# Two products a weight block for the queries, the memory keys and the convolution input, with a PSUM bank for each half

## The chip, the core and the metric

The kernel runs on one core of one Trainium2 chip. The core has a matrix engine (TensorE, PE in the profile), a vector engine (VectorE, DVE), a scalar engine (ScalarE, ACT), a general engine (GpSimd, POOL) and DMA queues, most of them issued by SyncE (SP). Each engine works through its own queue in order, and semaphores tie the queues together. Matrix products land in PSUM, eight banks of 512 fp32 columns a partition; everything else lives in SBUF. The metric is the time of one execution on the device, in microseconds (us), smaller being better.

## The reference: a trunk of two layers

A sequence of 256 tokens of width 1024 goes through two layers. Each layer has four steps, each followed by a layer norm of the sum with the residual:

```
x <- LN(alpha*x + 0.5*SwiGLU_1(x))
x <- LN(alpha*x + W_o( sum_b sigmoid(G_b x) * (y_b W_b) ))     b in {retention, DSA, NSA, SSD}
x <- LN(alpha*x + CrossAttn(x, mem))                           4 heads, 256 memory tokens
x <- LN(alpha*x + 0.5*SwiGLU_2(x))
```

Three places matter here. The cross attention projects queries from `x` and keys from `mem`, both 1024 wide. The SSD mixer takes 768 of its input columns through a causal convolution of four taps and a SiLU:

```
q = (x @ wq).reshape(B, S, X_HEADS, X_DH)
kv = (mem @ wkv).reshape(B, M, 2, X_HEADS, X_DH)
xbc = silu(conv(xbc, conv_w) + conv_b)
```

The NSA mixer compresses its keys into 15 blocks and scores every query of four heads against them:

```
p_cmp = masked_softmax(jnp.einsum('bshd,bcd->bhsc', q, k_cmp) * scale, cmp_visible[None, None])
```

Everything is fp32, and the kernel has to keep close to fp32 precision.

## The kernel before

**Precision by halves.** TensorE multiplies numbers of a reduced type (`F32R`) in one pass. The kernel therefore writes every operand as a high part and a low part: ScalarE copies the number into the reduced type (`wH`, line 177; line 207 for activations), VectorE subtracts that from the original (`wL`, line 178; line 208). A product is the sum of high by high, high by low and low by high. The helper `mm3` (lines 188 to 193) issues these as three matmuls into one PSUM region.

**Weights.** All weights stream once from HBM, most of the 267 MB read, in chunks of 1 MB. `chunk_hl` issues the load into one of three `raw` buffers, and splits it in two halves of 128 x 1024, each into a `wH` and a `wL` from a pool that holds four such pairs, that is, two chunks. So a later chunk's split has to wait until TensorE has used up a half two chunks earlier, and its load until a `raw` buffer is free.

**Units.** The work of TensorE is cut into generators, "units", each of which uses one weight chunk. The next unit's chunk is loaded and split while the current one multiplies. Between units' pieces, the small steps of the token mixers, of the attention heads and of the layer norms are woven in. A scheduler at build time then sets the order of instructions in each engine's queue; it is fixed when the kernel runs.

**Features by tokens.** `feat2` (line 417) computes 256 output features for 256 tokens, as two feature tiles `ft` of 128 rows. Both go into one PSUM bank of the pair called `mm`: columns 0 to 255 for the first, 256 to 511 for the second. For each tile there are eight weight blocks of 128 x 128, and for each block three matmuls of 256 columns: `wH` by `xH` (line 191), `wH` by `xL` (192), `wL` by `xH` (193). When both tiles are done, the bank is read once. Four kinds of unit use it. In a layer there are

- four memory-key units (`kv_unit`, line 440, for i < 4), whose bank ScalarE copies into `kT` (line 200);
- four `query` units (line 537), whose bank ScalarE scales into `qH` (line 544) and VectorE reads again for `qL` (line 545);
- three `conv` units (line 1023), whose bank ScalarE copies into `xp` (line 200); VectorE then computes the taps into `cu` (lines 1036 and 1038), ScalarE a tanh (`cth`, 1040), VectorE the result `xc` (1042);
- sixteen gate units, which the change doesn't touch.

The memory-key units fill TensorE while a layer norm runs on VectorE: four in the first norm of layer 0, and for layer 1 two each in the third and fourth norms of layer 0. In the cross attention each query unit is followed by a head's steps, woven into the next query's: scores into a bank of the pair `tp` (`tp<-xkH,qH` and its like), softmax, transposes and values.

The feed-forward units have another form (lines 369 and 370): `xH` and `xL` lie beside each other in the tile `xP`, so `wH` is multiplied with both in one matmul of 512 columns, and `wL` by `xH` is added to the first 256. The bank then holds two halves, which ScalarE copies (374) and VectorE adds (375).

**Scores on compressed keys.** In `nsa` the compressed keys `kcT` are one fp32 tile of 128 x 16, and each of eight matmuls (two token tiles, four heads; line 979) is a full fp32 product, whose result VectorE adds to a mask (line 985).

**Around the convolution.** The SSD mixer's scan is woven into the convolution units. There TensorE multiplies a table `sA` with ones (line 1095), VectorE turns a column of that into `ncs` (1088, 1105), and TensorE adds a mask to the same bank (1109), for which it waits for `ncs`.

Of the kernel before, what the change touches and what calls it, by code (L numbers as in the profile page):

```python
# [9 lines left out]
F32 = mybir.dt.float32  # L10
F32R = mybir.dt.float32r
BF16 = mybir.dt.bfloat16
AF = mybir.ActivationFunctionType
# [3 lines left out]
S = 256  # L17
# [121 lines left out]
class Trunk:  # L139
# [277 lines left out]
    def feat2(self, sp, x, first=None):  # L417
# [8 lines left out]
                    yield  # L426
        return b


    def load_mem(self, pool, tag="mem"):  # L430
        both = pool.tile([128, 2, 8, S], F32R, name="mem", tag=tag, bufs=1)
        self.memH, self.memL = both[:, 0], both[:, 1]
        r = self.rawp.tile([128, 2048], F32, name="raw")
        self.nc.sync.dma_start(r, self.a["memT"])
        for i in range(2):
            sl = slice(4 * i, 4 * i + 4)
            self.hl_from(self.memH[:, sl].rearrange("p a b -> p (a b)"),
                         self.memL[:, sl].rearrange("p a b -> p (a b)"), r[:, i * 1024:(i + 1) * 1024])

    def kv_unit(self, l, i):  # L440

        if i == 0:
            self.kT = self.big.tile([128, 8, S], F32, name="kT")
            self.vM = self.big.tile([128, 2, D], F32, name="vM")
        mem = lambda k, sl=slice(0, S): (self.memH[:, k, sl], self.memL[:, k, sl])
        sp = self.chunk_hl(l, "kv"[i // 4], i % 4)
        yield
        if i < 4:
            b = yield from self.feat2(sp, mem)
            self.evac(self.kT[:, 2 * i:2 * i + 2, :].rearrange("p a b -> p (a b)"), b, eng="act")  # L450
            return
        hf, part = divmod(i - 4, 2)
        if part == 0:
            self.vacc = [self.mmb() for _ in range(2)]
        for kk in range(4):
            k = part * 4 + kk
            w = tuple(p[:, (kk % 2) * 512:(kk % 2) * 512 + 512] for p in sp[kk // 2])
            for t in range(2):
                self.mm3(self.vacc[t], mem(k, slice(t * 128, t * 128 + 128)), w, k == 0, k == 7)
            yield  # L460
        if part == 1:
            for t in range(2):
                self.evac(self.vM[:, t, hf * 512:hf * 512 + 512], self.vacc[t], eng="act")
# [73 lines left out]
    def query(self, l, h, wk):  # L537
        nc = self.nc
        sp = self.chunk_hl(l, "q", h)
        yield  # L540
        b = yield from self.feat2(sp, self.x_hl)
        self.q[h] = [wk[0].tile([128, 2, S], F32R, name="q" + n) for n in "HL"]
        qH, qL = (w.rearrange("p a b -> p (a b)") for w in self.q[h])
        nc.scalar.activation(qH, b, AF.Copy, scale=1.0 / 16.0)
        nc.vector.scalar_tensor_tensor(qL, b, 1.0 / 16.0, qH.bitcast(F32), op0=OP.mult, op1=OP.subtract)

    def token_acc(self, acc, blocks, first, last):

# [368 lines left out]
    def nsa(self, mp):  # L917
# [46 lines left out]
        nc.tensor.matmul(cp[0][:, :16], w2r.rearrange("p a b -> p (a b)"), x[:, 0, :], start=True, stop=True)  # L964
        nc.tensor.matmul(cp[1][:64, :64], rep.rearrange("p a b -> p (a b)"), w2, start=True, stop=True)

        kcT = self.sm.tile([128, 16], F32, name="kcT", bufs=1)
        nc.scalar.activation(kcT, cp[0][:, :16], AF.Copy)
        vb = mp.tile([128, 4, 64], F32, name="vblk", bufs=1)
        nc.gpsimd.memset(vb[64:], 0.0)  # L970
        bm = self.c("blkm", 64)
# [3 lines left out]
        sc = self.acc()  # L975
        for t in range(2):
            for h in range(4):
                c = (t * 4 + h) * 16
                nc.tensor.matmul(sc[:, c:c + 16], nqT[t][:, h].bitcast(F32), kcT, start=True, stop=True)
        pc = self.sm.tile([128, 2, 4, 16], F32, name="pc", bufs=1)  # L980
        mx = self.sm.tile([128, 8], F32, name="pcm", bufs=1)
        sm = self.sm.tile([128, 8], F32, name="pcs", bufs=1)
        cm = self.c("cmpm").rearrange("p (t o c) -> p t o c", t=2, o=1)
        pc3 = pc.rearrange("p t h c -> p (t h) c")
        nc.vector.tensor_tensor(pc, sc[:, :128].rearrange("p (t h c) -> p t h c", t=2, h=4), cm.to_broadcast([128, 2, 4, 16]), OP.add)
        nc.vector.tensor_reduce(mx, pc3, axis=AX, op=OP.max)
        nc.vector.tensor_scalar(mx, mx, -0.1 * BIG, None, op0=OP.max)
        nc.vector.tensor_tensor(pc3, pc3, mx[:, :, None].to_broadcast([128, 8, 16]), OP.subtract)
# [34 lines left out]
    def conv(self, l, i, mp):  # L1023

        nc = self.nc
        sp = self.chunk_hl(l, "xbc", i)
        yield
        b = yield from self.feat2(sp, self.x_hl)
        xp = mp.tile([128, 2, S + 3], F32, name="xp", tag="t2")
        nc.gpsimd.memset(xp[:, :, :3], 0.0)  # L1030
        self.evac(xp[:, :, 3:], b.rearrange("p (a n) -> p a n", a=2), eng="act")
        u = mp.tile([128, 2, S], F32, name="cu", tag="t2")
        cw = self.cwh[:, :24].rearrange("p (f j) -> p f j", f=6)
        for a in range(2):
            f = 2 * i + a
            nc.vector.tensor_scalar(u[:, a], xp[:, a, 3:], cw[:, f, 3:4], self.cwh[:, 24 + f:25 + f], op0=OP.mult, op1=OP.add)
            for j in range(3):
                nc.vector.scalar_tensor_tensor(u[:, a], xp[:, a, j:j + S], cw[:, f, j:j + 1], u[:, a], op0=OP.mult, op1=OP.add)
        th = mp.tile([128, 2, S], F32, name="cth", tag="t2")
        nc.scalar.activation(th, u, AF.Tanh)  # L1040
        xc = mp.tile([128, 2, S], F32, name=f"xc{i}", bufs=1)
        nc.vector.scalar_tensor_tensor(xc, th, 1.0, u, op0=OP.add, op1=OP.mult)
        self.xc[i] = xc
        if i == 2:
            self.done.add("xbc")
# [383 lines left out]
```

## Time and profile before

| | us |
|---|---|
| median of three runs | 1471.2 |
| lowest and highest run | 1469.06, 1472.23 |
| profiled execution | 1470.16 |
| its span, first to last instruction | 1468.4 |
| TensorE busy | 1451.9 (99%) |
| VectorE busy | 1059.1 (72%) |
| ScalarE busy | 800.4 (55%) |
| GpSimd busy | 126.1 (9%) |

The granted TensorE clock was 0.998 of full speed over the span. The busy time of a matmul in the profile includes its way through a pipeline, so matmuls overlap: 128 x 256 products are listed with some 0.28 us and start 0.12 us apart. What a stream of them costs is read from start to start. An idle time in brackets is that of the engine before the instruction, with what ended it.

### The profile page before, as it was taken

The page shows a single profiled execution, that of the slowest core. Times are in us where ns is not written, and L with a number is a line of the kernel's source. Part 1 is how long each engine was busy: PE and PEld are TensorE (multiplying, and loading weights), DVE is VectorE, ACT ScalarE, POOL GpSimd, SP SyncE. Part 2 cuts the span into 40 slices and gives each one's busy share as a digit, 9 for nine tenths or more (in the row PEclk, how much of TensorE's full clock was granted, in tenths as well). Part 3 has the DMA queues.
Part 4 walks back from the last instruction along what each step waited for, and adds up shares of the span by engine and source line. Part 5 has one row for each costly group of instructions (what it writes and reads, how often), then busy time and mean ns, then how long its engine had stood idle before and what let it go on. Part 6 is the DMA issues. An engine that isn't in the chain of part 4 may idle for free.

```text
span 1468.4 us, 22627 instructions
## 1 busy us (share of the span) xinstructions
PE 1451.9 (99%) x8949; PEld 1292.0 (88%) x8949; DVE 1059.1 (72%) x1671; ACT 800.4 (55%) x1302; POOL 126.1 (9%) x130
## 2 busy tenths in 40 slices
PE   8999999999999999999999999999999999999997
PEld 6888899899997988888898888898999979888886
DVE  7666668887768777666676566789877788676665
ACT  6555546645654546555546565466556546365552
POOL 0000002301421000000000000023014210000000
PEclk9999999999999999999999999999999999999999
DMA  8576555543454636555556555454333555365550
GB/s 311 190 275 237 189 165 188 172 132 128 144 187 183 234 144 227 186 210 191 190 176 224 191 209 179 179 200 172 121 139 144 192 180 203 115 230 182 208 184 29
DMA packets 40857, 269.38 MB, mean 183 GB/s; under 512 B 4528, under 2 KB 4784, under 8 KB 10288
## 3 DMA queue, kind: packets, MB, share of 16 engines
q1 hardware_dynamic: 40176, 266.89, 51.4%
q8 instruction: 70, 1.15, 0.3%
q10 hardware_dynamic: 576, 1.05, 0.2%
q14 instruction: 35, 0.29, 0.1%
HBM read 266.88 MB, written 1.05 MB: 182 GB/s over the span
## 4 chain that ended last, share of the span: by engine, by line
PE 96%; DVE 1%; DMA 1%; ACT 1%; POOL 0%; issue 0%; DVEq 0%; ACTq 0%
PE tp L369 11%; PE mm L369 11%; PE acc L193 10%; PE acc L191 10%; PE acc L192 10%; PE mm L191 8%; PE mm L192 8%; PE mm L193 8%; PE mm L370 5%; PE tp L370 5%; PE tp L327 1%; PE tp L192 1%; PE tp L681 1%; PE tp L193 1%; PE tp L191 1%; PE tp L603 1%
## 5 line engine op out<-in xcount | busy, mean ns | idle before, releaser
L178 DVE TENSOR_TENSOR wL<-raw,wH 128x1024 fp32r<-128x1024 f32 (+2 forms) x478 | 585.3, 1233 | 235.4 <-ACT wH L177 231.6
L177 ACT ACTIVATE wH<-raw 128x1024 fp32r<-128x1024 f32 (+2 forms) x478 | 496.1, 1048 | 300.4 <-PE mm L192 127.3
L369 PE MATMUL mm<-xP,wH 128*128 128x512 f32 x704 | 249.4, 394 | 1.8 <-DVE xP L208 1.8
L369 PE MATMUL tp<-xP,wH 128*128 128x512 f32 x704 | 249.1, 394 | 0.0
L191 PE MATMUL mm<-xP,wH 128*128 128x256 f32 x736 | 213.9, 291 | 0.3 <-ACT vM L200 0.3
L192 PE MATMUL mm<-xP,wH 128*128 128x256 f32 x736 | 208.5, 283 | 0.0
L193 PE MATMUL mm<-xP,wL 128*128 128x256 f32 x736 | 208.0, 283 | 0.0
L370 PE MATMUL mm<-xP,wL 128*128 128x256 f32 x704 | 195.7, 278 | 0.5 <-DVE wL L178 0.5
L370 PE MATMUL tp<-xP,wL 128*128 128x256 f32 x704 | 195.4, 278 | 0.0
L369 PEld LDWEIGHTS mm<-xP,wH 128*128 128x128 f32 x704 | 132.0, 187 | 33.6 <-ACT wH L177 2.5
L369 PEld LDWEIGHTS tp<-xP,wH 128*128 128x128 f32 x704 | 132.0, 188 | 30.7
L191 PEld LDWEIGHTS mm<-xP,wH 128*128 128x128 f32 x736 | 140.6, 191 | 2.3 <-ACT vM L200 1.4
L192 PEld LDWEIGHTS mm<-xP,wH 128*128 128x128 f32 x736 | 140.6, 191 | 1.4 <-issue 0.6
L193 PEld LDWEIGHTS mm<-xP,wL 128*128 128x128 f32 x736 | 140.6, 191 | 0.1
L192 PE MATMUL acc<-wL,hH 128*128 128x512 f32 x352 | 137.8, 392 | 0.0
L191 PE MATMUL acc<-wH,hH 128*128 128x512 f32 x352 | 137.7, 391 | 0.0
L193 PE MATMUL acc<-wH,hL 128*128 128x512 f32 x352 | 137.5, 391 | 0.0
L370 PEld LDWEIGHTS mm<-xP,wL 128*128 128x128 f32 x704 | 132.3, 188 | 5.0 <-DVE wL L178 1.6
L370 PEld LDWEIGHTS tp<-xP,wL 128*128 128x128 f32 x704 | 132.3, 188 | 0.0
L374 ACT ACTIVATE g<-mm 128x256 f32<-128x256 f32 x88 | 33.7, 383 | 111.4 <-PE mm L370 111.3
L375 DVE TENSOR_TENSOR g<-mm,g 128x256 f32<-128x256 f32 x88 | 37.2, 423 | 75.2 <-ACT g L374 75.2
L193 PE MATMUL acc<-wH,xP 128*128 128x512 f32 (+1 forms) x224 | 85.0, 379 | 1.9 <-POOL xP L1198 1.9
(332 smaller groups left out, 2385.8 us busy)
## 6 DMA issues: line engine op xcount, KB each, us to landing
raw<-in_w_dram SPq DMA_DIRECT2D x232, 1024.0 KB, 4.9
raw<-in_memT_dram SPq DMA_DIRECT2D x5, 1024.0 KB, 4.8
lnG<-in_ln_g_dram SPq DMA_DIRECT2D x8, 512.0 KB, 3.8
lnB<-in_ln_b_dram SPq DMA_DIRECT2D x8, 512.0 KB, 5.1
raw<-in_w_dram SPq DMA_DIRECT2D x4, 624.0 KB, 3.9
w<-in_w_dram SPq DMA_DIRECT2D x8, 256.0 KB, 4.8
raw<-in_w_dram SPq DMA_DIRECT2D x4, 256.0 KB, 6.2
raw<-in_xT_dram ACTq DMA_DIRECT2D x4, 256.0 KB, 6.6
```

The lines of the kernel that those rows point to most:

```text
L177: self.nc.scalar.activation(h, src, AF.Copy)
L178: self.nc.vector.tensor_tensor(lo, src, h.bitcast(F32), OP.subtract)
L191: mm(out, a[0], b[0], start=start, stop=False, **kw)
L192: mm(out, a[0], b[1], start=False, stop=False, **kw)
L193: mm(out, a[1], b[0], start=False, stop=stop, **kw)
L327: nc.tensor.transpose(p[:, k * 128:k * 128 + 128], X[:, t, (h * 4 + k) * 128:(h * 4 + k + 1) * 128], self.ident)
L369: nc.tensor.matmul(b[s], w[0][:, off:off + 128], self.xP[:, :, k], start=k == 0, stop=False, skip_group_check=True)
L370: nc.tensor.matmul(b[s][:, :256], w[1][:, off:off + 128], self.xH[:, k], start=False, stop=k == 7, skip_group_check=True)
L374: nc.scalar.activation(g[:, s], b[s][:, 256:], AF.Copy)
L375: nc.vector.tensor_tensor(g[:, s], b[s][:, :256], g[:, s], OP.add)
L603: self.nc.tensor.transpose(p[:parts, i * 128:i * 128 + 128].bitcast(F32R), v, self.identr)
L681: nc.tensor.transpose(b[:, h * 128:h * 128 + 128], ps[h // hb][:, h % hb, j * 128:j * 128 + 128], self.ident)
```

## The change

A new generator `feat_apart` takes the place of `feat2` for memory keys, queries and convolution inputs. It gives each of the two feature tiles a whole `mm` bank, and uses two matmuls a weight block, in the form of the feed-forward units: 512 columns of `[xH | xL]` with `wH`, and 256 columns of `xH` with `wL`. After each feature tile the bank's two halves are put together by `both`: ScalarE copies the one, VectorE adds the other. For queries this goes into one small fp32 buffer `half`, which is then split into `qH` and `qL` as any other activation. The compressed keys are split as well: the scores have `F32R` operands and 32 columns (16 high, 16 low), and a second VectorE operation adds the two.

```diff
+    def feat_apart(self, sp, xP, evac):
+        nc = self.nc
+        for ft in range(2):
+            b = self.mmb()
+            for k in range(8):
+                h, lo = (p[:, k * 128:k * 128 + 128] for p in sp[ft])
+                nc.tensor.matmul(b, h, xP[:, :, k], start=k == 0, stop=False, skip_group_check=True)
+                nc.tensor.matmul(b[:, :256], lo, xP[:, 0, k], start=False, stop=k == 7, skip_group_check=True)
+                if k == 7:
+                    evac(ft, b[:, :256], b[:, 256:])
+                if k % 4 == 3:
+                    yield
+
+    def both(self, out, high, low, scale=1.0):
+        self.nc.scalar.activation(out, low, AF.Copy, scale=scale)
+        self.nc.vector.scalar_tensor_tensor(out, high, scale, out, op0=OP.mult, op1=OP.add)
...
         if i < 4:
-            b = yield from self.feat2(sp, mem)
-            self.evac(self.kT[:, 2 * i:2 * i + 2, :].rearrange("p a b -> p (a b)"), b, eng="act")
+            kT = self.kT[:, 2 * i:2 * i + 2]
+            yield from self.feat_apart(sp, self.memP, lambda ft, b, lo: self.both(kT[:, ft], b, lo))
             return
...
         sp = self.chunk_hl(l, "q", h)
         yield
-        b = yield from self.feat2(sp, self.x_hl)
-        self.q[h] = [wk[0].tile([128, 2, S], F32R, name="q" + n) for n in "HL"]
-        qH, qL = (w.rearrange("p a b -> p (a b)") for w in self.q[h])
-        nc.scalar.activation(qH, b, AF.Copy, scale=1.0 / 16.0)
-        nc.vector.scalar_tensor_tensor(qL, b, 1.0 / 16.0, qH.bitcast(F32), op0=OP.mult, op1=OP.subtract)
+        def evac(ft, b, lo):
+            if ft == 0:
+                self.q[h] = [wk[0].tile([128, 2, S], F32R, name="q" + n) for n in "HL"]
+            t = self.sm.tile([128, S], F32, name="half", bufs=1)
+            self.both(t, b, lo, 1.0 / 16.0)
+            self.hl_from(*(w[:, ft] for w in self.q[h]), t)
+
+        yield from self.feat_apart(sp, self.xP, evac)
...
-        kcT = self.sm.tile([128, 16], F32, name="kcT", bufs=1)
-        nc.scalar.activation(kcT, cp[0][:, :16], AF.Copy)
+        kcT = self.sm.tile([128, 2, 16], F32R, name="kcT", bufs=1)
+        self.hl_from(kcT[:, 0], kcT[:, 1], cp[0][:, :16])
...
-                c = (t * 4 + h) * 16
-                nc.tensor.matmul(sc[:, c:c + 16], nqT[t][:, h].bitcast(F32), kcT, start=True, stop=True)
+                c = (t * 4 + h) * 32
+                nc.tensor.matmul(sc[:, c:c + 32], nqT[t][:, h], kcT.rearrange("p a c -> p (a c)"), start=True, stop=True)
...
-        nc.vector.tensor_tensor(pc, sc[:, :128].rearrange("p (t h c) -> p t h c", t=2, h=4), cm.to_broadcast([128, 2, 4, 16]), OP.add)
+        scv = sc[:, :256].rearrange("p (t h a c) -> p t h a c", t=2, h=4, a=2)
+        nc.vector.tensor_tensor(pc, scv[:, :, :, 0], cm.to_broadcast([128, 2, 4, 16]), OP.add)
+        nc.vector.tensor_tensor(pc, scv[:, :, :, 1], pc, OP.add)
...
-        b = yield from self.feat2(sp, self.x_hl)
         xp = mp.tile([128, 2, S + 3], F32, name="xp", tag="t2")
         nc.gpsimd.memset(xp[:, :, :3], 0.0)
-        self.evac(xp[:, :, 3:], b.rearrange("p (a n) -> p a n", a=2), eng="act")
+        yield from self.feat_apart(sp, self.xP, lambda ft, b, lo: self.both(xp[:, ft, 3:], b, lo))
```

In the changed file the two matmuls are lines 437 and 438 and the two operations of `both` lines 445 and 446; later lines move by 22 to 24, so that what was line 1038 is 1062, and 1105 is 1129.

Since the scheduler sets the order again, rows move beside each other. The first place is VectorE's queue at the first two queries of layer 0. Before, from the split of the first head's keys and values on:

```order
L208 TENSOR_TENSOR xvL<-vM,xvH 128x512
L178 TENSOR_TENSOR wL<-raw,wH 128x1024 x2
L545 SCALAR_TENSOR_TENSOR qL<-mm,qH 128x512
L178 TENSOR_TENSOR wL<-raw,wH 128x1024 x2
L488 TENSOR_REDUCE xnm<-tp 128x2
```

After, from the same row on:

```order
L208 TENSOR_TENSOR xvL<-vM,xvH 128x512
L178 TENSOR_TENSOR wL<-raw,wH 128x1024
L446 SCALAR_TENSOR_TENSOR half<-mm,half 128x256
L178 TENSOR_TENSOR wL<-raw,wH 128x1024
L208 TENSOR_TENSOR qL<-half,qH 128x256
L178 TENSOR_TENSOR wL<-raw,wH 128x1024
L446 SCALAR_TENSOR_TENSOR half<-mm,half 128x256
L178 TENSOR_TENSOR wL<-raw,wH 128x1024
L208 TENSOR_TENSOR qL<-half,qH 128x256
```

One operation of a query has become four, with splits of weights between them. ScalarE's queue at the same place, before:

```order
L207 ACTIVATE xkH<-kT 128x512
L207 ACTIVATE xvH<-vM 128x512
L177 ACTIVATE wH<-raw 128x1024 x2
L544 ACTIVATE qH<-mm 128x512
L177 ACTIVATE wH<-raw 128x1024 x3
```

And after:

```order
L207 ACTIVATE xkH<-kT 128x512
L207 ACTIVATE xvH<-vM 128x512
L177 ACTIVATE wH<-raw 128x1024
L445 ACTIVATE half<-mm 128x256
L177 ACTIVATE wH<-raw 128x1024
L207 ACTIVATE qH<-half 128x256
L177 ACTIVATE wH<-raw 128x1024
L445 ACTIVATE half<-mm 128x256
L177 ACTIVATE wH<-raw 128x1024 x2
```

The second copy out of a bank now comes after the third of these splits, where the one copy of before came after the second. The last place is VectorE's queue at the first convolution unit of layer 0, before:

```order
L202 CAST iqT<-tp 128x512
L178 TENSOR_TENSOR wL<-raw,wH 128x1024
L1088 TENSOR_SCALAR ncs<-acc 128x8
L1105 TENSOR_TENSOR ncs<-acc,ncs 128x4
L1036 TENSOR_SCALAR cu<-xp,cwh 128x256 x2
L1038 SCALAR_TENSOR_TENSOR cu<-xp,cwh,cu 128x256 x6
```

And after:

```order
L202 CAST iqT<-tp 128x512
L178 TENSOR_TENSOR wL<-raw,wH 128x1024
L446 SCALAR_TENSOR_TENSOR xp<-mm,xp 128x256
L1112 TENSOR_SCALAR ncs<-acc 128x8
L1129 TENSOR_TENSOR ncs<-acc,ncs 128x4
L1060 TENSOR_SCALAR cu<-xp,cwh 128x256
L1062 SCALAR_TENSOR_TENSOR cu<-xp,cwh,cu 128x256 x2
L446 SCALAR_TENSOR_TENSOR xp<-mm,xp 128x256
L1062 SCALAR_TENSOR_TENSOR cu<-xp,cwh,cu 128x256
L1060 TENSOR_SCALAR cu<-xp,cwh 128x256
L178 TENSOR_TENSOR wL<-raw,wH 128x1024
```

The add of the first feature tile stands ahead of `ncs`, and the taps of that tile no longer wait for the second one.

## Rows read from the trace of the kernel before

**Rows 1.** Page: busy time of each engine, and the chain by engine.

```profile
PE 1451.9 (99%) x8949; PEld 1292.0 (88%) x8949; DVE 1059.1 (72%) x1671; ACT 800.4 (55%) x1302; POOL 126.1 (9%) x130
...
PE 96%; DVE 1%; DMA 1%; ACT 1%; POOL 0%; issue 0%; DVEq 0%; ACTq 0%
```

**Rows 2.** By stretch: length; PE, PEld, DVE, ACT, POOL busy; clock; DMA share, GB/s.

```profile
546.00:559.00 13.00, 13.00 (x111) 12.91 (x111) 12.63 (x21) 5.72 (x8) 1.85 (x2) 1.00 0.30 89
...
226.00:262.00 36.00, 35.74 (x242) 32.86 (x241) 31.78 (x69) 22.39 (x41) 9.65 (x10) 1.00 0.46 150
...
487.00:520.00 33.00, 33.00 (x269) 32.26 (x268) 25.55 (x38) 23.15 (x40) 0.00 (x0) 1.00 0.51 182
1208.00:1241.00 33.00, 32.70 (x266) 31.73 (x265) 28.53 (x40) 22.77 (x40) 0.00 (x0) 1.00 0.65 228
```

**Rows 3.** Timeline of PE (start, duration, operation): old triples, query and memory.

```profile
488.21 0.28 PE L191 MATMUL mm<-xP,wH 128*128 128x256 f32 x1
...
493.60 0.28 PE L191 MATMUL mm<-xP,wH 128*128 128x256 f32 x1
...
204.06 0.28 PE L191 MATMUL mm<-mem,wH 128*128 128x256 f32 x1
...
215.06 0.28 PE L191 MATMUL mm<-mem,wH 128*128 128x256 f32 x1
```

**Rows 4.** Timeline of PE: pairs of two feed-forward units.

```profile
64.17 0.39 PE L369 MATMUL tp<-xP,wH 128*128 128x512 f32 x1
...
66.59 0.40 PE L369 MATMUL tp<-xP,wH 128*128 128x512 f32 x1
...
755.31 0.39 PE L369 MATMUL mm<-xP,wH 128*128 128x512 f32 x1
...
758.14 0.40 PE L369 MATMUL tp<-xP,wH 128*128 128x512 f32 x1
```

**Rows 5.** Timeline of PE: compressed scores, and neighbours of 256 columns.

```profile
346.03 0.28 PE L649 MATMUL acc<-keyH,qT 128*128 128x256 f32 x1
346.15 0.28 PE L650 MATMUL acc<-keyL,qT 128*128 128x256 f32 x1
...
346.74 1.85 PE L979 MATMUL acc<-kcT,qT 128*128 128x16 f32 x16
348.44 0.36 PE L191 MATMUL mm<-xP,wH 128*128 128x256 f32 x1
```

**Rows 6.** Page, costliest groups: busy us, mean ns of one, idle before.

```profile
L178 DVE TENSOR_TENSOR wL<-raw,wH 128x1024 fp32r<-128x1024 f32 (+2 forms) x478 | 585.3, 1233 | 235.4 <-ACT wH L177 231.6
L177 ACT ACTIVATE wH<-raw 128x1024 fp32r<-128x1024 f32 (+2 forms) x478 | 496.1, 1048 | 300.4 <-PE mm L192 127.3
...
L374 ACT ACTIVATE g<-mm 128x256 f32<-128x256 f32 x88 | 33.7, 383 | 111.4 <-PE mm L370 111.3
L375 DVE TENSOR_TENSOR g<-mm,g 128x256 f32<-128x256 f32 x88 | 37.2, 423 | 75.2 <-ACT g L374 75.2
```

**Rows 7.** Timeline of ACT at the first two queries of either layer.

```profile
493.68 1.06 ACT L177 ACTIVATE wH<-raw 128x1024 fp32r<-128x1024 f32 x1 [1.82 <-PE mm L192]
...
495.46 3.11 ACT L177 ACTIVATE wH<-raw 128x1024 fp32r<-128x1024 f32 x3 [0.23 <-DMA raw<-in_w_dram]
...
1216.88 1.06 ACT L177 ACTIVATE wH<-raw 128x1024 fp32r<-128x1024 f32 x1 [1.77 <-PE mm L192]
...
1218.77 2.96 ACT L177 ACTIVATE wH<-raw 128x1024 fp32r<-128x1024 f32 x3 [0.35 <-DMA raw<-in_w_dram]
```

**Rows 8.** Timeline of PE and DVE at the first convolution unit, layer 0.

```profile
240.56 0.38 PE L1109 MATMUL acc<-lowb,nident 128*128 128x512 bf16 x1 [0.26 <-DVE ncs L1105]
...
242.64 0.74 DVE L1036 TENSOR_SCALAR cu<-xp,cwh 128x256 f32<-128x256 f32 x2 [2.13 <-ACT xp L200]
```

**Rows 9.** Timeline of DVE at the norm's end; PE's waits, sum, times, longest.

```profile
558.38 1.29 DVE L208 TENSOR_TENSOR xP<-tp,xP 128x512 fp32r<-128x512 f32 x2 [0.29 <-ACT xP L207]
...
PE mm L369 <- DVE xP L208: 1.8, 3, 0.8
```

More of the change, by code (lines that the diff above doesn't have):

```diff
@@ L427, in feat2 @@
         return b
+    def feat_apart(self, sp, xP, evac):
[13 more added lines that the diff above has]
+        self.nc.vector.scalar_tensor_tensor(out, high, scale, out, op0=OP.mult, op1=OP.add)
     def load_mem(self, pool, tag="mem"):
         both = pool.tile([128, 2, 8, S], F32R, name="mem", tag=tag, bufs=1)
-        self.memH, self.memL = both[:, 0], both[:, 1]
+        self.memP, self.memH, self.memL = both, both[:, 0], both[:, 1]
         r = self.rawp.tile([128, 2048], F32, name="raw")
```

## The prediction

> **What bounds the kernel now.** I read the page's totals first, then the chain of work that ended last, then the stages in which the changed units run. TensorE is busy 99% of the span and makes up 96% of the chain [rows 1]: it is the bound, and it runs its queue in a fixed order. So only two things move the time: how long the matmul queue is, and where its head has to wait. VectorE, at 72%, has room on average; but the change puts work on it in four kinds of stage, and there the room differs [rows 2]: 28.5 of 33 us in the queries of layer 1, 25.6 of 33 in those of layer 0, 31.8 of 36 in the convolution, 12.6 of 13 in the norm beside which two memory-key units run. Those stages decide.
>
> **What it takes from TensorE.** Busy times of matmuls overlap, so I cost a block by its start-to-start distance. The old three products of 256 columns over xP: 15 blocks lie between the query's first complete block at 488.21 and the next query's first at 493.60, 5.39/15 = 359 ns [rows 3]. The same over the memory: 31 blocks from 204.06 to 215.06, 11.00/31 = 355 ns [rows 3]. The new form, one product of 512 columns and one of 256, is what the feed-forward units already do: 7 blocks from 64.17 to 66.59 give 346 ns, 8 from 755.31 to 758.14 give 354 [rows 4]. The form is the same, the place differs, so I take the middle, 350. Fourteen units over xP (8 queries, 6 convolution inputs) of 16 blocks save 224 x 9 ns = 2.0 us (1.1 at 354, 2.9 at 346); eight memory-key units save 128 x 5 ns = 0.6 us (0.1 to 1.2).
>
> The scores on compressed keys: 16 records start between 346.74 and 348.44, 1.70 us a layer, two records for each of the 8 fp32 matmuls [rows 5]. With split keys 8 single products are left. At the same 106 ns apiece they cost 0.85, and their neighbours with 256 columns, 120 ns apart [rows 5], bound them by 0.96: 0.85 less a layer, 1.7 in all (1.5 to 1.9). The split of the keys (one more small VectorE operation) and the second add hang on a woven chain with two yields before its matmuls; I cost them at nothing, and if that cover is gone, at two small operations of some 0.2 us a layer. Savings together: 2.0 + 0.6 + 1.7 = **4.3 us** (2.7 to 6.0).
>
> At this place the Trainium skill, TensorE: Matmul & The Clock Gate (Back-to-back issue gap), speaks against the change: it gives a matmul its columns over 2.4 GHz and about 2.5 ns beside, so that three products and two differ by 2.5 ns a block; over all 352 blocks that would be an estimated 0.9 us instead of 2.6. The rows show a larger difference, 1 to 13 ns.
>
> **What it adds elsewhere.** A half (256 columns of one feature tile) now leaves its bank by a ScalarE copy and a VectorE add, 0.38 and 0.42 us by the feed-forward rows of that form [rows 6], about 0.8 in a row. Before, a unit filled one bank and the next unit the other, so a bank had a whole unit, 16 x 359 ns = 5.7 us, to be emptied. Now it has the other half's 8 x 350 ns = 2.8 us. The 0.8 us fit easily; a queue in front of them may not, for the splits of weights (L177 1.05, L178 1.23 [rows 6]) stand in the same two queues. I went through the new order of each stage with the times of the trace.
>
> *Queries.* In layer 0 the first query's halves end on TensorE at about 490.6 and 493.4, the second's first half at about 496.2; three score products (0.36 us) later, at about 496.7, its second half wants the bank of the first query's second half. ScalarE's order now puts that half's copy behind the split that waited for its weights' DMA and began at 495.46 [rows 7]: the split ends at 496.5, the copy at 496.85. VectorE's add stands behind the low part of the same split, 496.5 to 497.7, and ends at about 498.1. TensorE waits 1.4 us. The single buffer of `half` forbids the copies to run ahead. With 0.15 us at the first half's bank and 0.25 for the scores of the second feature tile, whose qH stands behind two more splits, that is 1.8 us. In layer 1 the same split begins, again after a DMA, at 1218.77 behind a split at 1216.88 [rows 7]; the rows lie 723.2 to 723.3 later than those of layer 0, so the same 1.4 us appear. Besides, VectorE goes from one operation of 0.68 us a query to four of 0.42: four times 1.0 us on top of 28.5 of 33, so I add 0.5 there. Taken: 1.8 + 2.3 = **4.1 us** (1.6 if the copies slip in ahead of the DMA-bound split, 5.6 if later halves wait too).
>
> *Convolution.* The add into `xp` now stands ahead of `ncs`, for which TensorE waits already (0.26 us at 240.56 [rows 8]): +0.35. The `cu` chain gains, since its first half can start in the 2.13 us that VectorE sat idle before 242.64 [rows 8]. But the third convolution's first bank waits for the second's add, which stands behind `xc` and the tanh, ready between 249.0 and 249.45 where TensorE comes at 249.05; and the low part of a later projection's weights stands behind the last chain, up to 0.65 late. I take 0.35 + 0.3 + 0.35 = 1.0 a layer, **2.0 us** (0.8 to 3.0).
>
> *Norm with two key units.* Three adds get into a queue that is busy 12.6 of 13 us [rows 2], ahead of the `xP` parts (558.38, idle before them 0.29 [rows 9]) for which the next feed-forward's first matmul waits already, 1.8 us in three places [rows 9]. 3 x 0.42 less the idle time is 1.0; as other work is moved behind in turn, I take **0.6 us** (0 to 1.0). The other six key units have VectorE free when their halves end; what hides their adds is VectorE's idle time, and without it each costs the 0.4 of its add.
>
> **Sum.** -4.3 + 4.1 + 2.0 + 0.6 = +2.4 us. The profiled execution took 1470.2 us, which lies between the runs shown (1469.1 to 1472.2, median 1471.2): 1470.2 + 2.4 = 1472.6 us. With the ends of the terms the forecast's own range is -6.0 + 2.4 = -3.6 to -2.7 + 9.6 = +6.9; all terms at one end is unlikely.
>
> **Rivals.** *The waits don't come.* If the banks are empty in time, as VectorE's 72% and an evacuation of 0.8 in 2.8 us suggest, the savings stand alone: 1470.2 - 4.3 = 1465.9, faster by 0.3%. Against it: the split behind a DMA at 495.46 is a row, not an average.
>
> *VectorE becomes the bound of the changed stages.* Place: queries of layer 1, then convolution. Price: the upper ends, 5.6 + 3.0 + 1.0 - 4.3 = +5.3, 1475.5 us. It decides from where a half's add ends later than 2.8 us after its last matmul, that is, where two splits stand ahead of it. For it: 28.5 + 4.0 = 32.5 of 33 us, and 12.6 + 3 x 0.42 over 13. Against it: the splits themselves come no faster than DMA and TensorE free their buffers, so a late add is partly made up.
>
> *The pair isn't shorter here.* Two products stream the same 768 columns as three; at the 354 ns of 755.31 the blocks save 1.2 us instead of 2.6, and the sum is +3.8: 1474.0 us. For it: 354 against the memory's 355. Against it: 346 in the run at 64.17. By the Trainium skill's rule above (TensorE: Matmul & The Clock Gate, Back-to-back issue gap) it would be an estimated +4.1.
>
> **How the numbers follow.** Forecast 0.50, no waits 0.20, VectorE the bound 0.22, no shorter pair 0.08. A measurement of this kernel tells about 0.2% (2.9 us) from no change. Of the forecast's 0.50 I put 0.35 within that, 0.11 above, 0.04 below; no waits is faster; VectorE the bound is 0.20 slower, 0.02 same; the last 0.05 slower, 0.03 same. Faster 0.24, same 0.40, slower 0.36. The range must reach both outer cases: 1465.7, a little under no waits, leaves out about 0.1 below, and 1476.5, a little over VectorE the bound, about 0.1 above. The likeliest case alone reaches from 1468 to 1476.
>
> **What would show it.** Pairs at 346 to 354 ns start to start; 8 score products a layer in about 0.85 us; a TensorE wait of about 1.4 us on the add into `half` near 497 and 1220; 0.6 us before the scan's mask (L1109) near 240.6 and 976; the feed-forward after the cross attention starting about 0.6 us later against its norm. No wait on `half` at all would prove the main step wrong: then the first rival holds. So would copies that ScalarE reaches before the DMA-bound split. Waits of the feed-forward or projections on VectorE's low parts, away from the banks, would speak for the second rival.

## The result: 0.7% slower

The changed kernel's median is 1481.65 us (six runs, 1478.4 to 1483.16) against 1470.83 for the kernel before in the same session (six runs): a ratio of 1.0072, 95% interval 1.0060 to 1.0083, about +10.8 us. The forecast of 1472.6 us was 9 us short, and the time lies above the range. The profiled execution took 1480.12 us, its span 1478.3, at a granted clock of 0.998 as before.

The page of the changed kernel: busy time of PE, the chain by engine, then two of the costliest groups (busy us, mean ns of one, idle before).

```profile
PE 1458.7 (99%) x8581; PEld 1278.2 (86%) x8581; DVE 1075.2 (73%) x1727; ACT 809.0 (55%) x1340; POOL 131.1 (9%) x130
...
PE 93%; DVE 4%; DMA 1%; ACT 1%; issue 1%; POOL 0%; DVEq 0%; ACTq 0%
...
L369 PE MATMUL mm<-xP,wH 128*128 128x512 f32 x704 | 254.2, 400 | 1.7 <-DVE xP L208 1.7
...
L437 PE MATMUL mm<-xP,wH 128*128 128x512 f32 x224 | 81.7, 403 | 4.7 <-DVE half L446 3.6
```

TensorE has 368 instructions fewer than in [rows 1] and is busy 6.8 us longer. The first hint is line 369, the feed-forward pairs, which the diff doesn't touch: a matmul is listed with 400 ns, where the kernel before has 394:

```profile
L369 PE MATMUL mm<-xP,wH 128*128 128x512 f32 x704 | 249.4, 394 | 1.8 <-DVE xP L208 1.8
```

The waits of TensorE after (sum, times, longest, us):

```profile
PE mm L437 <- DVE half L446: 3.6, 2, 2.4
...
PE mm L369 <- DVE xP L208: 1.7, 3, 0.8
PE mm L437 <- DVE xP L208: 0.9, 1, 0.9
...
PE acc L193 <- POOL xP L1222: 0.7, 2, 0.3
```

The two waits on `half` are there, as forecast, but all waits listed for TensorE sum to 10.7 us, where the kernel before has 7.7: 3 us more, not 10. So I read where the two traces drift apart.

**Where the time goes.** Take the start of the same untouched matmul in both traces. The marks are the first and the last `wL` by `hH` product of layer 0's second feed-forward. Such a product of the hidden halves (`hH`, `hL`) and the down weights, the last matrix of a feed-forward, is called a down product here. Kernel before:

```profile
576.60 0.39 PE L192 MATMUL acc<-wL,hH 128*128 128x512 f32 x1
...
741.75 0.39 PE L192 MATMUL acc<-wL,hH 128*128 128x512 f32 x1
```

and after:

```profile
579.02 0.40 PE L192 MATMUL acc<-wL,hH 128*128 128x512 f32 x1
...
746.10 0.39 PE L192 MATMUL acc<-wL,hH 128*128 128x512 f32 x1
```

165.15 us became 167.08, in a stage with the same instructions in the same order and hardly a wait. The other three feed-forward stages grow by the same 1.9. Worked out like this, from the shift of such marks in each trace (us, kernel less kernel before; the last three columns are experiments told of below):

| stretch | after | e1_layout | e2_after_old_layout | e8_no_queries |
|---|---|---|---|---|
| start, to the first down product | +1.0 | +0.4 | +0.2 | +0.5 |
| four feed-forward stages | +7.7 | +7.7 | 0.0 | 0.0 |
| scores on compressed keys, 2 layers | -1.8 | +0.1 | -1.8 | -1.8 |
| late mixing, layer 0 | -1.1 | -1.0 | -1.3 | -1.4 |
| queries, layer 0 | +1.5 | 0.0 | +1.6 | 0.0 |
| norm behind them | +0.4 | -0.5 | +0.4 | +0.5 |
| queries, layer 1 | +2.9 | -0.1 | +7.2 | +1.5 |
| all else | -0.7 | -0.1 | -0.4 | -0.7 |
| end of the trace | +9.9 | +6.5 | +5.9 | -1.4 |

So the touched stages come to little, and the untouched ones carry the loss. The two traces lie 9.9 us apart and the medians 10.8: the profiled execution is the second shortest of its six. The four longer ones have a mean granted clock of 0.996 or 0.997, the two shorter ones 0.998; what the clock did in the longer ones no trace shows.

The unit of the first run in [rows 4] shows what they lose. After (PE timeline: the first, the ninth and the last of its 16 pairs):

```profile
62.83 0.39 PE L369 MATMUL mm<-xP,wH 128*128 128x512 f32 x1
...
65.66 0.40 PE L369 MATMUL tp<-xP,wH 128*128 128x512 f32 x1
...
68.12 0.40 PE L369 MATMUL tp<-xP,wH 128*128 128x512 f32 x1
```

15 pairs in 5.29 us are 353 ns each; the kernel before has 346 there [rows 4]. With 1408 pairs, 6.5 ns more on each would be 9.2 us; 7.7 are seen. The first three units of each of the last three feed-forward stages, which follow no down product, have 347 or one of the slower paces in either kernel (354 at 755.31 before [rows 4], 347 in the same unit after); the growth is in the units that follow down products.

### The profile page after: what moved, and what is told of

The parts are those of the page before. It is cut to its first block, busy times and chain, and to the rows that moved or that the text cites. A ratio compares the mean times of both kernels' runs of the same rounds, so it can differ in the third digit from the quotient of the medians.

```text
span 1478.3 us, 21979 instructions
## 1 busy us (share of the span) xinstructions
PE 1458.7 (99%) x8581; PEld 1278.2 (86%) x8581; DVE 1075.2 (73%) x1727; ACT 809.0 (55%) x1340; POOL 131.1 (9%) x130
## 4 chain that ended last, share of the span: by engine, by line
PE 93%; DVE 4%; DMA 1%; ACT 1%; issue 1%; POOL 0%; DVEq 0%; ACTq 0%
PE mm L369 11%; PE tp L369 11%; PE acc L193 10%; PE acc L192 10%; PE acc L191 10%; PE mm L370 6%; PE tp L370 6%; PE mm L191 6%; PE mm L192 5%; PE mm L193 5%; PE mm L437 4%; PE mm L438 2%; DMA raw<-in_w_dram 1%; DVE wL L178 1%; PE tp L327 1%
## 5 line engine op out<-in xcount | busy, mean ns | idle before, releaser
L369 PE MATMUL mm<-xP,wH 128*128 128x512 f32 x704 | 254.2, 400 | 1.7 <-DVE xP L208 1.7
L369 PE MATMUL tp<-xP,wH 128*128 128x512 f32 x704 | 253.3, 399 | 0.0
L370 PE MATMUL mm<-xP,wL 128*128 128x256 f32 x704 | 198.6, 282 | 0.8 <-DVE wL L178 0.8
L369 PEld LDWEIGHTS mm<-xP,wH 128*128 128x128 f32 x704 | 132.8, 189 | 34.8 <-DVE xP L208 1.7
L191 PE MATMUL mm<-xP,wH 128*128 128x256 f32 x512 | 149.5, 292 | 0.0
L192 PE MATMUL mm<-xP,wH 128*128 128x256 f32 x512 | 144.8, 283 | 0.0
L193 PE MATMUL mm<-xP,wL 128*128 128x256 f32 x512 | 144.6, 282 | 0.0
L370 PEld LDWEIGHTS mm<-xP,wL 128*128 128x128 f32 x704 | 133.5, 190 | 4.6 <-DVE wL L178 1.1
L191 PEld LDWEIGHTS mm<-xP,wH 128*128 128x128 f32 x512 | 97.7, 191 | 0.7
L192 PEld LDWEIGHTS mm<-xP,wH 128*128 128x128 f32 x512 | 97.8, 191 | 0.5
L193 PEld LDWEIGHTS mm<-xP,wL 128*128 128x128 f32 x512 | 97.6, 191 | 0.0
L437 PE MATMUL mm<-xP,wH 128*128 128x512 f32 x224 | 81.7, 403 | 4.7 <-DVE half L446 3.6
```

The lines of the kernel that those rows point to most:

```text
L191: mm(out, a[0], b[0], start=start, stop=False, **kw)
L192: mm(out, a[0], b[1], start=False, stop=False, **kw)
L193: mm(out, a[1], b[0], start=False, stop=stop, **kw)
L369: nc.tensor.matmul(b[s], w[0][:, off:off + 128], self.xP[:, :, k], start=k == 0, stop=False, skip_group_check=True)
L370: nc.tensor.matmul(b[s][:, :256], w[1][:, off:off + 128], self.xH[:, k], start=False, stop=k == 7, skip_group_check=True)
L437: nc.tensor.matmul(b, h, xP[:, :, k], start=k == 0, stop=False, skip_group_check=True)
```

## What could slow an untouched stage

The theory after the result: the change makes tiles in the pool `small` larger (`half`, 1024 B a partition, and 64 B more of `kcT`), so every tile of the pools behind it lies 1088 B further on in SBUF: the feed-forward's hidden halves and its down weights among them. In the built programs these start at 32 modulo 128 before and at 96 after. `xP` and the up weights, the operands of the pairs themselves, don't move. The rival: the second-order effects of a changed order (weights that arrive later, engines in another rhythm). The layout can be tried without the change, and the change without the layout.

**The layout alone: e1_layout.** The kernel before with an unused tile of 1088 B in `small`; the instructions and their order are those of before.

```diff
+        self.sm.tile([128, 272], F32, name="pad", bufs=1)
         b = yield from self.feat2(sp, self.x_hl)
```

> The kernel before with one unused tile of 1088 bytes a partition in the pool `small`, so that every tile behind that pool lies where it lies in the changed kernel; all five queues are the same row for row. Theory A, that the places of tiles in SBUF set the rhythm of the feed-forward's pairs: pairs go from 346 to 352-353 ns start to start, 1408 of them, so some +8 us, about 1479 us. Theory B, that the changed instruction stream sets it: pairs stay at 346 and the time at 1470.8.

Measured: 1476.77 us (four runs) against 1470.51, ratio 1.0043 (1.0027 to 1.0060), +6.3 us. First and last pair of the same unit:

```profile
62.14 0.39 PE L369 MATMUL mm<-xP,wH 128*128 128x512 f32 x1
...
67.44 0.40 PE L369 MATMUL tp<-xP,wH 128*128 128x512 f32 x1
```

5.30/15 = 353 ns, and the column of the table above: +7.7 us in the feed-forward stages, as in the changed kernel, and next to nothing in the stages of the change. A place alone costs what the change costs there. The whole is 2 us less than the 8 expected; the trace has 1.0 less in the late mixing and 0.5 less in a norm, which the pad doesn't explain.

**The change in the old layout: e2_after_old_layout.** `half` and `kcT` go into pools behind the others, so that the feed-forward's tiles lie where they did.

```diff
-            t = self.sm.tile([128, S], F32, name="half", bufs=1)
+            t = wk[0].tile([128, S], F32, name="half", bufs=1)
...
-        kcT = self.sm.tile([128, 2, 16], F32R, name="kcT", bufs=1)
+        self.sm.tile([128, 16], F32, name="pad", bufs=1)
+        kcT = mp.tile([128, 2, 16], F32R, name="kcT", bufs=1)
```

> The changed kernel with `half` in the pool of the cross attention and `kcT` in that of the mixers, so that the feed-forward's tiles lie where they lie in the kernel before; all five queues are those of the changed kernel. Theory A (places): pairs at 346 ns and about 1473.6 us, which leaves +2 to +3 us for the waits that the prediction summed. Theory B (instruction stream): pairs stay at 352.6 and the time at 1481.7.

Measured: 1474.57 us (six runs), ratio 1.0029 (1.0017 to 1.0040), +4.1 us; 6.7 us less than the changed kernel over before, by the places of tiles. The pairs are back at 346 ns (5.19/15):

```profile
61.55 0.39 PE L369 MATMUL mm<-xP,wH 128*128 128x512 f32 x1
...
66.74 0.40 PE L369 MATMUL tp<-xP,wH 128*128 128x512 f32 x1
```

What is left, +4.1, is what the instructions of the change cost in this layout. The profiled run, 1476.05, is the longest of the six, and shows why in the queries of layer 1 (below).

**Which places: e3_pad64, e4_pad1024, e7_pad32, e11_pad96.** The pad of e1_layout in other sizes: 64, 1024, 32 and 96 B.

```diff
+        self.sm.tile([128, 16], F32, name="pad", bufs=1)      # e4: 256, e7: 8, e11: 24
```

> The kernel before with an unused tile of 64 bytes in `small`; the same queues. Theory A: if the shift by 64 bytes (that of the wider `kcT`) is what counts, pairs at 352-353 ns and about 1479 us; if that of 1024 bytes counts, 346 ns and 1470.8. Theory B: 346 and 1470.8.

> The kernel before with an unused tile of 1024 bytes in `small`; the same queues. Theory A: 352-353 ns and about 1479 us if the shift by 1024 bytes (that of `half`) counts, else 346 and 1470.8. Theory B: 346 and 1470.8.

> The kernel before, with 32 unused bytes in `small`: the shifted tiles then start at 64 modulo 128 bytes, as xP and the split weights do, where they start at 32 in the kernel before and at 96 in the changed one; the same queues. If only a start at 96 is slow: pairs at 346 ns, about 1470.5 us. If a rhythm of its own belongs to each start: another value than 346 and 352.6. If any shift that is not a multiple of 128 is slow: 352.6 and 1476.5.

> The kernel before with 96 unused bytes in `small`, so that the shifted tiles start at 0 modulo 128 bytes; the same queues. If 32 is the one good start of the four: 352-353 ns a pair and about 1476 us. If 0 is another good one: 346 ns and about 1470 us.

**Which tiles: e5_pad64_down_weights and e6_pad64_h.** e5 puts 64 B ahead of the down weights alone. e6 puts 64 B ahead of the hidden halves as well, so that these start at 96 and the weights, moved by 128 B in all, at 32 again.

```diff
+        wk.tile([128, 16], F32, name="padwk", bufs=1)          # e6 only
+        dn.tile([128, 16], F32, name="paddn", bufs=1)
         quads = [(t, hf) for t in range(2) for hf in range(2)]
```

> The kernel before, with 64 unused bytes ahead of the down-projection weights of the feed-forward alone; g, h, hH and hL stay where they are; the same queues. Theory A1, the place of the streamed down weights sets the rhythm: pairs at 352.6 ns, about 1476.5 us. Theory A2, the place of hH and hL (loaded as weights by TensorE, written by ScalarE and VectorE) sets it: pairs at 346 ns, about 1470.5.

> The kernel before, with g, h, hH and hL moved by 64 bytes and the down weights by 128, which by the run with 1024 bytes should count as nothing; the same queues. A1 (down weights): pairs at 346 ns, about 1470.5 us. A2 (hH, hL): pairs at 352.6 ns, about 1476.5.

Measured, together with the others (time against the before of the same session; feed-forward: growth of the four stages as in the table above). Apart from e1 and e2 these are single runs, and the kernel before alone spreads from 1468.2 to 1472.9 us in one session, so the last column decides and not the time:

| kernel | hidden halves start, mod 128 | down weights start, mod 128 | time, us (less before) | feed-forward, us |
|---|---|---|---|---|
| before | 32 | 32 | | 0 |
| e4_pad1024 | 32 | 32 | 1471.21 (+0.7) | 0.0 |
| e2_after_old_layout | 32 | 32 | 1474.57 (+4.1) | 0.0 |
| e11_pad96 | 0 | 0 | 1471.88 (+2.6) | +1.0 |
| e6_pad64_h | 96 | 32 | 1470.56 (+1.1) | +0.9 |
| e5_pad64_down_weights | 32 | 96 | 1474.62 (+5.1) | +5.5 |
| e7_pad32 | 64 | 64 | 1476.65 (+7.2) | +6.8 |
| e3_pad64 | 96 | 96 | 1476.45 (+5.9) | +7.7 |
| e1_layout | 96 | 96 | 1476.77 (+6.3) | +7.7 |

The pad's size is not what counts: 1024 B cost nothing, 32 and 64 B cost as much as 1088. The start modulo 128 tells them apart, 0 and 32 on one side (with +1.0 for 0), 64 and 96 on the other. e5 and e6 part the tiles. Moving the hidden halves alone costs 0.9, all in the down products and nothing in the pairs. Moving the down weights alone, the operand that streams through TensorE in the products just ahead of the next pairs, costs 5.5: 1.6 in those products themselves and 3.9 in the pairs. Both together (e1) cost 7.7, all in the pairs, so the two don't simply add up, and e5's time lies between the two that were expected. In e5 the pace changes from unit to unit, a first unit of 16 pairs at 5.21/15 = 347 ns, the next with ten pairs in 3.52, 352 ns:

```profile
87.04 0.39 PE L369 MATMUL mm<-xP,wH 128*128 128x512 f32 x1
...
92.25 0.39 PE L369 MATMUL tp<-xP,wH 128*128 128x512 f32 x1
...
95.37 0.39 PE L369 MATMUL mm<-xP,wH 128*128 128x512 f32 x1
...
98.89 0.40 PE L369 MATMUL tp<-xP,wH 128*128 128x512 f32 x1
```

Two units in a row use different weight buffers and banks. But in the built programs of e1, e5 and e6 the operands and results of all 1408 pairs lie where they lie in the kernel before, and there both of these units have 346 ns. So the pace is set by what ran before, and then lasts for the unit.

A rival is that other engines, which write the moved tiles while the pairs run, slow them down. The last unit of e5 speaks against that. Its first and last pair, and the stretch (length; PE, PEld, DVE, ACT, POOL busy; clock; DMA share, GB/s):

```profile
1447.26 0.40 PE L369 MATMUL mm<-xP,wH 128*128 128x512 f32 x1
...
1452.56 0.40 PE L369 MATMUL tp<-xP,wH 128*128 128x512 f32 x1
```

```profile
1447.00:1453.00 6.00, 6.00 (x36) 5.20 (x35) 1.70 (x4) 1.61 (x4) 0.00 (x0) 1.00 0.00 0
```

No DMA runs, no weights are split any more, and the pairs still take 5.30/15 = 353 ns; no down products stand between this unit and the one before it, whose pace it keeps.

## What the change itself costs

**Without the queries: e8_no_queries.** e2 with the four query units of a layer in the old form; memory keys, convolution and scores stay changed.

```diff
-        yield from self.feat_apart(sp, self.xP, evac)
+        b = yield from self.feat2(sp, self.x_hl)
+        self.q[h] = [wk[0].tile([128, 2, S], F32R, name="q" + n) for n in "HL"]
+        qH, qL = (w.rearrange("p a b -> p (a b)") for w in self.q[h])
+        nc.scalar.activation(qH, b, AF.Copy, scale=1.0 / 16.0)
+        nc.vector.scalar_tensor_tensor(qL, b, 1.0 / 16.0, qH.bitcast(F32), op0=OP.mult, op1=OP.subtract)
```

> The changed kernel with the queries as they were (feat2, no `half`) and the feed-forward's tiles where they lay before: memory keys, convolution inputs and compressed keys are changed. If the waits of the queries are what is left of the loss once the places are put back: 1470.5 - 1.8 (scores) - 0.3 (keys, convolution) + 0.5 (norm) = about 1469 us. If the other units' banks lose as much as the prediction summed for them (+2.6, against 2.6 of savings that go with keys, convolution and scores): about 1470.5 us.

Measured: 1468.67 us (ten runs) against 1469.49, ratio 0.9989 (0.9979 to 0.9999): 0.8 us faster than before, just clear of no change. With the queries it was +4.1, so the queries cost some 4.9 us, and the three other parts together gain about one. Its trace is 1.5 us longer in the queries of layer 1 all the same, where the instructions are those of before. There the split behind the DMA starts at 1217.95, 1.8 us late for its stage, and TensorE waits at 1224.12 for the softmax:

```profile
PE tp L521 <- DVE p L515: 1.3, 1, 1.3
```

So a late load in that stage is not of the new queries alone.

**Queries with four banks: e9_queries_acc_banks.** e2, but the query's halves go to the four banks of `acc`, which the cross attention otherwise holds from its start and now takes at its first output product.

```diff
-    def feat_apart(self, sp, xP, evac):
+    def feat_apart(self, sp, xP, evac, bank=None):
...
-            b = self.mmb()
+            b = (bank or self.mmb)()
...
-        yield from self.feat_apart(sp, self.xP, evac)
+        yield from self.feat_apart(sp, self.xP, evac, self.acc)
```

> The changed kernel with the feed-forward's tiles where they lay before, and with the queries' halves in the four `acc` banks, which are free until the output products begin, in place of the two `mm` banks. If the queries lose by waiting for a bank behind a split that waits for its weights' DMA: no wait of L437 on `half` is left, the queries cost a little less than in their old form, and the time is 1474.6 - 5 to 6 = about 1469 us. If it is VectorE's and ScalarE's added operations that hold the heads back (four operations a query for one or two), the waits move to the scores and the time stays near 1473 to 1475.

Measured: 1468.36 us (ten runs) against 1469.32, ratio 0.9992 (0.9982 to 1.0001), which is 1.0 us under before where e2 was 4.1 above it. TensorE's waits:

```profile
PE tp L191 <- ACT qH L207: 1.5, 1, 1.5
PE tp L327 <- DVE X L312: 1.1, 1, 1.1
...
PE tp L521 <- DVE p L515: 0.6, 1, 0.6
```

No matmul waits for `half` any more. With two more banks the stall is gone; that shows the bank as its cause. Yet e9 is no faster than e8, which has the old queries. Its rows have new waits, on `qH` and on the residual's `X`, in which what the shorter query pairs save may be lost; no run parts the two.

**Scores alone: e12_scores_only and e13_scores_only_old_layout.** The kernel before with the split compressed keys, first as the change has them (64 B more in `small`), then in the old layout.

```diff
-        kcT = self.sm.tile([128, 16], F32, name="kcT", bufs=1)
-        nc.scalar.activation(kcT, cp[0][:, :16], AF.Copy)
+        kcT = self.sm.tile([128, 2, 16], F32R, name="kcT", bufs=1)          # e13: a 64 B pad here, kcT in mp
+        self.hl_from(kcT[:, 0], kcT[:, 1], cp[0][:, :16])
...
+                nc.tensor.matmul(sc[:, c:c + 32], nqT[t][:, h], kcT.rearrange("p a c -> p (a c)"), start=True, stop=True)
```

> The kernel before with the compressed keys split and nothing else, as the change writes it, so that `kcT` takes 64 bytes more. By the places' theory: 1470 - 1.7 for the scores + 6 for the shift by 64 bytes = about 1474.5 us, pairs at 352.6 ns. By the sum of the prediction alone: about 1468.5, pairs at 346.

> The same, with `kcT` in the mixers' pool and the 64 bytes of before left in `small`, so that the feed-forward's tiles lie as before; the same queues as in the run with the split alone. Places: about 1468.5 us, pairs at 346 ns. If splitting the keys itself costs what the other run loses: as that one.

Measured, one run each against 1469.32: 1475.08 (+5.8) and 1467.33 (-2.0). The same arithmetic is a loss with 64 B ahead of the down weights (feed-forward stages +7.7) and a gain without (0.0). This is the smallest edit that shows it. Of the two times the gain is the less certain: it lies 1.0 us under the lowest of the 13 runs of the kernel before.

## Why the prediction was wrong, step by step

**The step that failed** is the premise of the sum, "So only two things move the time: how long the matmul queue is, and where its head has to wait". By it the sum counts the touched stages and puts every other matmul at nothing. But the pace at which unchanged matmuls follow each other moved as well. The four feed-forward stages cost +7.7 us, by tiles that the change moved and that no line of the diff names. The clue stood in [rows 4]: one form, 346 ns in one unit and 354 in another. I put that to the place of the unit in the program and took the middle for the new pairs, instead of asking what makes an identical instruction slower, and whether the change could move 1408 others from the one pace to the other. The formula that I set beside it, the Trainium skill, TensorE: Matmul & The Clock Gate (Back-to-back issue gap), has columns and a fixed gap alone, and the section gives it for an isolated matmul; worked out from it, an estimated 325 ns lie between the starts of two pairs, wherever the tiles lie. Here the measurement decides: e1_layout has 353 ns for the 346 of before, with the same columns.

The rest of the trace, 9.9 - 7.7 = +2.2, with 1.0 of the start (0.2 in e2, which has the same instructions) and -1.1 of the late mixing in it, is near the sum's +2.4. That is in part luck: against the sum the queries cost 1.5 more and the convolution 1.2 less. Its terms:

**Pairs instead of triples: direction right, size uncertain.** Memory keys, PE timeline, after:

```profile
199.28 0.39 PE L437 MATMUL mm<-mem,wH 128*128 128x512 f32 x1
...
204.48 0.39 PE L437 MATMUL mm<-mem,wH 128*128 128x512 f32 x1
```

15 pairs in 5.20 us, 347 ns each, for 355 before [rows 3]; but over `xP` 347 to 354, by unit. The middle of 350 was fair. The rival of the pair that isn't shorter fails for the memory keys, but in the new layout only: there `mem` has moved too, and in e2, where it lies as before, the last memory-key unit of the first norm has 354 ns a pair.

**Scores: right, a little small.** After, all eight products and the next instruction:

```profile
349.08 1.15 PE L1001 MATMUL acc<-kcT,qT 128*128 128x32 f32 x8
350.07 0.36 PE L191 MATMUL mm<-xP,wH 128*128 128x256 f32 x1
```

0.99 us from start to start, where [rows 5] has 1.70 for 16: 0.7 less by these rows (0.85 forecast; the bound of 120 ns apiece was nearer than 106), 0.9 by the marks around the stage. A product takes 124 ns from start to start, a little over that bound.

**Queries: the mechanism right, layer 1 mis-sized.** Layer 0 after, the instructions that the prediction named (ACT, DVE, PE):

```profile
495.93 1.06 ACT L177 ACTIVATE wH<-raw 128x1024 fp32r<-128x1024 f32 x1 [0.48 <-DMA raw<-in_w_dram]
...
496.89 0.36 ACT L445 ACTIVATE half<-mm 128x256 f32<-128x256 f32 x1
...
497.02 1.22 DVE L178 TENSOR_TENSOR wL<-raw,wH 128x1024 fp32r<-128x1024 f32 x1 [0.29 <-ACT wH L177]
...
498.16 0.42 DVE L446 SCALAR_TENSOR_TENSOR half<-mm,half 128x256 f32<-128x256 f32 x1
...
498.64 0.50 PE L437 MATMUL mm<-xP,wH 128*128 128x512 f32 x1 [1.23 <-DVE half L446]
```

The split behind the DMA, the copy behind the split, the add behind the low part, the bank behind the add: 1.23 us, for 1.4 in the working. The whole stage became 1.5 us longer; the sum's terms for it are 1.8 of stalls less half of the eight queries' 1.15, so +1.2. Layer 1:

```profile
1224.96 1.06 ACT L177 ACTIVATE wH<-raw 128x1024 fp32r<-128x1024 f32 x1 [1.64 <-DMA raw<-in_w_dram]
...
1225.92 0.36 ACT L445 ACTIVATE half<-mm 128x256 f32<-128x256 f32 x1
...
1227.19 0.42 DVE L446 SCALAR_TENSOR_TENSOR half<-mm,half 128x256 f32<-128x256 f32 x1
...
1227.66 0.50 PE L437 MATMUL mm<-xP,wH 128*128 128x512 f32 x1 [2.35 <-DVE half L446]
```

The same chain, 2.35 us. I took layer 1 as layer 0 plus 723.2 us, the load with it. But the load starts when a split frees a `raw` buffer, and lands by its own time. The chain of waits, after and then in e2_after_old_layout:

```profile
1218.88 6.05 DMA raw<-in_w_dram
```

```profile
1212.71 7.75 DMA raw<-in_w_dram
```

Against before's split at 1218.77 [rows 7], that of after comes 6.2 us later, where the matmuls ahead of the stage come 5.0 us later, so 1.2 late: 1.4 + 1.2 = 2.6, and the trace has 2.35. In e2 it starts at 1220.48, 1.7 later behind matmuls that come 1.2 us earlier, 2.9 late: 1.4 + 2.9 = 4.3, and the trace has 4.04. Why the load takes 6.05 us here and 7.75 there stays open. The second thing missed is at the stage's head: the old first product takes `xH` alone, the pair takes `xH` and `xL` at once, and so waits for VectorE's last low part. Before, then after:

```profile
1210.92 0.39 PE L191 MATMUL mm<-xP,wH 128*128 128x256 f32 x1 [0.30 <-ACT vM L200]
```

```profile
1216.14 0.47 PE L437 MATMUL mm<-xP,wH 128*128 128x512 f32 x1 [0.91 <-DVE xP L208]
```

0.6 us more. With both, the stage costs 2.9 where the sum has 2.3 - 0.6 = 1.7.

**Convolution: wrong, nothing instead of 1.1.** The sum has 2.0 for it, less 96 x 9 ns = 0.9 for its pairs. From the last projection product ahead of it to the projections behind it the shift against before goes from +2.58 to +2.53 us in layer 0 and from +5.69 to +5.67 in layer 1, and in e2 it changes as little (-0.01 to -0.05, -0.29 to -0.35). The wait of 0.26 [rows 8] is gone, not 0.6. I had counted each add put ahead of `ncs` at its full price, and the earlier start of the `cu` chain at nothing, though I had named it. The third part of the term is there: in the projection behind layer 0's convolution the product with the low part at 262.98 starts 0.36 us after the one before it and the next 0.34, for 0.23 among their neighbours, so 0.24 us are lost, for 0.35.

**Norm with two key units: right.** +0.4 to the marks behind it; 0.6 forecast, less the 0.16 that the pairs in it save by the sum.

**The rivals.** VectorE as the bound had the right sign, but not the reason: in the changed stages it has room as before. By stretch after (length; PE, PEld, DVE, ACT, POOL busy; clock; DMA share, GB/s), convolution and layer 1's queries, beside [rows 2]:

```profile
226.00:262.00 36.00, 35.90 (x195) 30.37 (x194) 32.02 (x75) 21.33 (x43) 9.81 (x13) 1.00 0.49 173
...
1217.00:1250.00 33.00, 30.31 (x193) 26.94 (x192) 28.13 (x48) 22.85 (x47) 0.00 (x0) 1.00 0.56 195
```

VectorE 28.1 of 33, for 28.5 before; the forecast of 32.5 was too high, as the stage became longer and 33 us of it hold a smaller part. The first rival, that the waits don't come, holds only where the banks are four (e9), and even there the time is 1.0 us under before and not 4.3.

**Not of the change.** The late mixing of layer 0 runs 1.0 to 1.4 us shorter in all four traces of the table, e1_layout too, which has nothing changed there. The kernel before has a wait on GpSimd in its trace that the others have in part (0.7 us after):

```profile
PE acc L193 <- POOL xP L1198: 1.9, 2, 1.5
```

So a term of that size in one trace isn't a term of the change.

## What to carry to other kernels

A new tile costs more than its instructions: it moves whatever lies behind it in SBUF, and here 64 B were worth 6 us of 1470. Before a change is judged, hold the layout of the untouched operands still (put new tiles behind them), and compare the pace of untouched matmuls in both traces first. A bank that is emptied by engines which also split weights behind a DMA is free only after that DMA; give such a product more banks; keeping its copy ahead of the split may do as well, which no run tried.

## What the runs showed of the chip

**Matmuls keep a pace that an earlier operand's place sets.** Same instructions, same operands: 346 or 347 ns a pair with the down weights at 0 or 32 modulo 128, 353 with them and the hidden halves at 64 or 96; with the weights alone at 96, 353 and 347 in turn. The down products themselves start 228 to 230 ns apart on average in each of these traces. What carries the pace from one product to the next stays open.

**A stall can cost twice.** In e2 the granted clock fell while TensorE stood idle for 4.04 us in the second query of layer 1. The matmul, and then the windows (length; PE busy, count; clock; DMA share, GB/s):

```profile
1223.18 0.80 PE L437 MATMUL mm<-xP,wH 128*128 128x512 f32 x1 [4.04 <-DVE half L446]
```

```profile
1222.00:1224.00 2.00, 0.81 (x3) 0.50 0.14 57
...
1226.00:1228.00 2.00, 2.00 (x10) 0.50 0.61 115
...
1230.00:1235.00 5.00, 4.66 (x31) 1.00 0.35 92
```

At 0.50, the lower level of 1.2 GHz, TensorE worked on from 1223.18 to about 1228.5; half of those 5.3 us, some 2.6, are the price. That is why this stage is +7.2 in e2 and +2.9 in the changed kernel (1.7 of longer wait and 2.6 of clock lie between them), whose 2.35 us idle left the clock at 1.00:

```profile
1224.00:1226.00 2.00, 1.31 (x9) 1.00 0.52 74
1226.00:1228.00 2.00, 0.34 (x1) 1.00 0.89 377
```

The length of one stall alone doesn't decide. In e4_pad1024 a stall of 1.46 us on GpSimd in layer 0's late mixing, after 0.32 us of another, was followed by the lower clock (PE busy, count; clock; DMA share, GB/s):

```profile
442.00:444.00 2.00, 2.00 (x6) 0.50 0.06 20
```

The kernel before has the same 1.46 us there, and 1.00 in the same stretch.

The other five runs of e2 were 0.4 to 2.4 us shorter than the profiled one; whether the clock fell in them no trace shows.
